# A whole row of output tile 36, instead of half a row, goes out by its own four small transfers

## The chip, the core and the metric

The kernel runs on one core of a Trainium2 chip, from one launch. The metric is the device time of an execution in microseconds (us), the median of several runs. The core has four compute engines that matter here (PE, the matmul engine; DVE, ACT and POOL, the elementwise engines), the engine SP, which only issues transfers, and 16 DMA engines that move data between the chip's main memory (HBM) and the on-chip memory of 128 partitions. DMAs that SP issues go through one queue (q1 in the profile), those that ACT issues through another (q10); every one of the 16 DMA engines serves both.

## What is computed

```python
x: (8, 12, 512, 64) float32      # batch, heads, rows t, channels c
y: (8, 12, 512, 64) float32
out = np.einsum('bhtc,bhsc->bhts', x, y)     # (8, 12, 512, 512) float32
```

These are 96 independent products, a 512x64 matrix by a 64x512 one. The inputs are 25.2 MB and the output is 100.7 MB, so most of the traffic is the output.

## The kernel before, in words

**Tiling.** The inputs come in twelve tiles of 128 partitions by 4096 float32 (16 KB a partition), six of x and six of y (`load`, line 129). ACT, DVE and POOL cast them to bfloat16 (`compress`, line 138), rearrange them (`mix`, line 162) and transpose them (`transposes`, line 177). The output is 48 tiles `o` of 128 partitions by 8 x 512 float32. A tile covers two heads. Partition p of it holds eight successive rows of one head, so that its 16 KB are one contiguous piece of HBM.

**One output tile** (`result`, line 259) is made in two halves, rows 0 to 3 and rows 4 to 7. For each half, PE does four matmuls of 128 by 512 (`products`, line 199, the matmul on line 205) into one of two PSUM buffers `pm0` and `pm1`. Then ACT copies the buffer into one of five `slot` buffers (line 115, the helper `copy`). In tiles 43 and 47 DVE copies in its place (line 117). After the second half the tile is stored by one DMA of 128 partitions by 16 KB (`store`, line 249, the issue on line 254): by SP, or, for every third tile and for the last four, by ACT, which then issues it after the first copy of the next tile.

**Order.** The program is written out by hand, tile after tile. `emit` (line 88) puts each operation on its engine's stream, and `need` (line 73) adds the semaphore waits that the buffers ask for. An engine runs its stream in order, so an operation that waits holds back all that stands behind it on that engine. A slot can be filled anew only when the DMA that stores it has landed.

**Tile 36 is the exception** (`SPLIT`, line 47). Its big store leaves out the last 256 of each partition's 4096 numbers (`size`, line 246), that is, the second half of the eighth row of every partition. These 128 pieces of 1 KB are computed again in another layout by `corner` (line 211), which `result` calls right after it has issued the big store. In `corner`:

- PE does eight matmuls (line 221) with 16 of the 128 rows each, by 256 columns, so that the result stands in 16 partitions by 2048 numbers of `pm0`.
- ACT copies that to `kept`, the first 16 partitions of a bfloat16 buffer that is no longer in use, `xk1` (line 230; the profile calls it xk<-pm).
- SP issues four DMAs (line 235). DMA r takes partitions r, r+4, r+8 and r+12 and writes eight pieces of 1 KB from each, 32 KB in all.

After that `result` goes on with tile 37. At the end of the program POOL waits for the four small DMAs (line 324), and the engines wait for the last store from each slot (lines 325 and 326).

Of the kernel before, what the change touches and what calls it, by code (L numbers as in the profile page):

```python
# [9 lines left out]
def kernel(  # L10
# [24 lines left out]
    _, _, S, _ = y.shape  # L35
    P = 128
    G = 16
# [5 lines left out]
    K = 8  # L43
# [1 line left out]
    D = 32  # L45
    SLOTS = 5
    SPLIT = 36
    W = S // 2
    fp32 = mybir.dt.float32
    bf16 = mybir.dt.bfloat16  # L50
    u32 = mybir.dt.uint32
# [5 lines left out]
    ov = out.rearrange("b h t s -> (b h t s)").rearrange(  # L57
        "(o u h q n) -> o h q u n", u=2, h=V, q=Q * E, n=K * S
    )
# [4 lines left out]
    xks = [sb.tile([P, R, C], bf16, name=f"xk{i}") for i in range(NG - 1)]  # L64
# [4 lines left out]
    pms = [ps.tile([P, 4, S], fp32, name=f"pm{i}") for i in range(2)]  # L69
# [18 lines left out]
    def emit(name, make, reads=(), writes=(), dma=None):  # L88

        points = [writer[r] for r in (*reads, *writes) if r in writer]  # L90
        points += [v for w in writes for v in readers.get(w, ())]
        if name == "pool" and name in ticks:
            points.append((name, ticks[name]))
        need(name, points)
        p, step = (name, 1) if dma is None else (f"dma{dma}", 16)
        if p not in sems:
            sems[p] = tc.alloc_semaphore(p)
        make().then_inc(sems[p], step)
        at = (p, ticks.get(p, 0) + step)
        ticks[p] = at[1]  # L100
        snaps[at] = {**known[name], p: at[1]}
        if dma is None:
            snaps[at][name] = at[1]
        for r in reads:
            readers.setdefault(r, []).append(at)
        for w in writes:
            writer[w], readers[w] = at, []
# [4 lines left out]
    def copy(name, dst, src, reads, writes):  # L112
        emit(
            name,
            lambda: nc.scalar.activation(dst, src, COPY)  # L115
            if name == "act"
            else engines[name].tensor_copy(dst, src),  # L117
            reads,
            writes,
        )  # L120
# [78 lines left out]
    def products(o, k):  # L199
        i, h = divmod(o, V)  # L200
        xT = xTs[i % 2].bitcast(bf16).rearrange("p (k h m) -> p k h m", k=K, h=V)
        yT = yTs[i % 2].bitcast(bf16)
        n = lambda j: min(S, size(o) - (k + j) * S)
        for j in range(4):
            last = nc.tensor.matmul(  # L205
                pms[k // 4][:, j, :n(j)], xT[:, k + j, h, :], yT[:, h * S:h * S + n(j)],
                start=True, stop=True,
            )
        return last

    def corner(o):

        i, h = divmod(o, V)
        xT = xTs[i % 2].bitcast(bf16).rearrange("p (k h m) -> p k h m", k=K, h=V)
        yT = yTs[i % 2].bitcast(bf16)
        kept = xks[1].bitcast(fp32).rearrange("p r c -> p (r c)")[:G, :]

        def make():

            for j in range(P // G):  # L220
                last = nc.tensor.matmul(  # L221
                    pms[0][:G, j // 2, j % 2 * W:(j % 2 + 1) * W],
                    xT[:, K - 1, h, j * G:(j + 1) * G],
                    yT[:, (h + 1) * S - W:(h + 1) * S],
                    start=True, stop=True,
                )
            return last

        emit("pe", make, [("xT", i % 2), ("yT", i % 2)], [("pm", 0)])
        copy("act", kept, pms[0].rearrange("p j s -> p (j s)")[:G, :], [("pm", 0)], [("xk", 1)])  # L230
        dst = ov[i, h].rearrange("(j a m) u n -> u m a j n", j=P // G, a=4)
        for r in range(4):
            emit(
                "sp",
                lambda: nc.sync.dma_start(
                    dst[r % 2, r // 2][:, :, K * S - W:],
                    kept[r::4].rearrange("p (j w) -> p j w", w=W),
                ),
                reads=[("xk", 1)],
                dma="corner",  # L240
            )
# [4 lines left out]
    def size(o):  # L246
        return K * S - W if o == SPLIT else K * S

# [10 lines left out]
    def result(o, s):  # L259

        for k in range(0, K, 4):
            pm = k // 4
            half = o // V % 2
            emit("pe", lambda: products(o, k), [("xT", half), ("yT", half)], [("pm", pm)])
            end = min(4 * S, size(o) - k * S)
            copy(
                "dve" if o in late else "act",
                slots[s][:, k * S:k * S + end],
                pms[pm].rearrange("p j s -> p (j s)")[:, :end],
                [("pm", pm)],  # L270
                [("slot", s, pm)],
            )
            if k == 0:
                while later:
                    store(*later.pop())
        if by_act(o):
            later.append((o, s))
        else:
            store(o, s)
        if o == SPLIT:  # L280
            corner(o)
# [75 lines left out]
```

## Time and profile before

| what | value |
|---|---|
| time, median of 3 runs | 300.77 us (300.7, 300.77, 301.01) |
| span of the profiled execution, first to last instruction | 298.9 us |
| what lies around the span, by the median of the runs | 1.87 us |
| bytes moved | 125.90 MB in 8789 packets, mean 421 GB/s |
| busiest compute engine | ACT, 205.4 us, 69% of the span |
| last landing of a transfer in the trace | 297.80 us |

The page gives no time of the profiled execution other than its span. So the 1.87 us is the difference between the median of the runs and the span, and it is taken to be the same for both kernels.

To read the profile: the slices on the page cut the span into 40 equal parts of 7.5 us and give the busy share of each engine in tenths. The DMA row is the mean over the 16 DMA engines. A DMA packet is one contiguous piece that one DMA engine moves; each transfer also has one packet of 4 bytes on every DMA engine that it uses, which reports the landing to a semaphore. The trace holds each packet's queue, start, duration and size, but not the number of its DMA engine.

### The profile page before, as it was taken

To read this page: it belongs to the slowest core of one execution; us is meant where nothing else is said; L and a number is where in the kernel's file an instruction comes from. 1 tells how busy PE (TensorE), PEld (TensorE's weight loads), DVE (VectorE), ACT (ScalarE), POOL (GpSimd) and SP (SyncE) were. 2 spreads that over 40 slices of the span, in tenths; PEclk is the share of its full clock that TensorE was granted. 3 is DMA by queue.
4 is the path that set the end of the run, shared out by engine and by line. 5 is a ranking of instruction groups with operands and counts; after the bars stand their busy time and mean duration, and the time that the engine had idled before them with its cause. 6 is when DMAs were issued, how large, how long until landed. Compare 5 with 4: busy or idle time off the path is not lost.

```text
span 298.9 us, 1185 instructions
## 1 busy us (share of the span) xinstructions
PE 128.5 (43%) x385; PEld 36.1 (12%) x392; DVE 160.7 (54%) x77; ACT 205.4 (69%) x106; POOL 56.1 (19%) x23
## 2 busy tenths in 40 slices
PE   0000040547566554464554555554653754567000
PEld 0000010111111111111111111111111211112000
DVE  2157897999839591920946719319377070500500
ACT  1665576999999876677776868685857994559000
POOL 2399999991000000000000000000000000000000
PEclk9999995657799979685979685959695799775655
DMA  7999999999999999999999999999999999999996
GB/s 274 430 423 439 430 428 423 428 439 428 425 436 432 425 425 442 428 428 432 432 428 433 434 428 425 436 425 428 434 434 425 422 433 419 423 428 425 430 434 259
DMA packets 8789, 125.90 MB, mean 421 GB/s; under 512 B 976, under 2 KB 1104, under 8 KB 1104
## 3 DMA queue, kind: packets, MB, share of 16 engines
q1 hardware_dynamic: 6192, 88.08, 69.4%
q10 hardware_dynamic: 2592, 37.75, 29.6%
q8 instruction: 3, 0.05, 0.1%
q14 instruction: 2, 0.02, 0.0%
HBM read 25.17 MB, written 100.66 MB: 421 GB/s over the span
## 4 chain that ended last, share of the span: by engine, by line
DMA 56%; ACT 22%; PE 7%; issue 5%; DVE 3%; SPq 0%; ACTq 0%
DMA out_dram<-slot 42%; ACT slot L115 19%; DMA slot<-in_y_dram 7%; DMA slot<-in_x_dram 6%; PE pm L205 6%; ACT xk L115 2%; DVE yb L117 2%; DVE slot L117 2%; ACT yb L115 1%; PE pm L221 1%; SPq L133 0%; ACTq L83 0%; SPq L352 0%; SPq L291 0%
## 5 line engine op out<-in xcount | busy, mean ns | idle before, releaser
L115 ACT ACTIVATE slot<-pm 128x2048 f32<-128x2048 f32 x92 | 166.0, 1884 | 47.9 <-DMA out_dram<-slot 38.2
L205 PE MATMUL pm<-yT,xT 128*128 128x512 bf16 x377 | 126.6, 475 | 144.3 <-ACT slot L115 96.3
L182 DVE STREAM_TRANSPOSE xT<-xb 128x2048 uint32<-128x2048 uint32 x12 | 46.7, 3888 | 75.3 <-PE pm L205 73.0
L205 PEld LDWEIGHTS pm<-yT,xT 128*128 128x128 bf16 x384 | 35.2, 111 | 235.4 <-ACT slot L115 134.9
L117 DVE COPY xb<-xk 32x2048 bf16<-32x2048 bf16 x36 | 46.9, 1302 | 1.0
L117 DVE CAST yb<-slot 64x2048 bf16<-64x2048 f32 x12 | 36.1, 3012 | 16.9 <-DMA slot<-in_y_dram 16.6
L117 POOL COPY xb<-xk 32x2048 bf16<-32x2048 bf16 x12 | 36.2, 3019 | 10.4 <-ACT xk L115 9.6
L115 ACT ACTIVATE xk<-slot 128x4096 bf16<-128x4096 f32 x6 | 21.7, 3617 | 16.3 <-DMA slot<-in_x_dram 16.2
L191 DVE STREAM_TRANSPOSE yT<-yb 128x1024 uint32<-128x1024 uint32 x12 | 23.1, 1922 | 0.0
L117 DVE COPY slot<-pm 128x2048 f32<-128x2048 f32 x4 | 9.0, 2286 | 25.3 <-PE pm L205 25.3
L115 ACT ACTIVATE yb<-slot 64x2048 bf16<-64x2048 f32 x6 | 14.8, 2461 | 5.1 <-DMA slot<-in_y_dram 5.1
L117 POOL CAST yb<-slot 64x2048 bf16<-64x2048 f32 x6 | 17.8, 2972 | 1.3 <-DMA slot<-in_y_dram 0.8
L221 PE MATMUL pm<-yT,xT 128*16 128x256 bf16 x8 | 1.9, 416 | 4.3 <-ACT slot L115 4.3
L297 DVE MEMSET xb<- 128x2048 uint32 x1 | 1.8, 1765 | 1.4 <-SPq L291 1.4
L115 ACT ACTIVATE xk<-pm 16x2048 f32<-16x2048 f32 x1 | 1.9, 1866 | 0.4 <-PE pm L221 0.4
L115 ACT ACT_TABLE_LOAD x1 | 1.3, 1283 | 0.9 <-SPq L291 0.9
L297 POOL MEMSET xb<- 128x2048 uint32 x1 | 1.8, 1804 | 0.5 <-SPq L291 0.5
L221 PEld LDWEIGHTS pm<-yT,xT 128*16 128x16 bf16 x8 | 0.9, 126 | 5.2 <-ACT slot L115 4.7
L341 POOL MEMSET const-float32-0.0<- 128x1 f32 x1 | 0.1, 97 | 0.2 <-issue 0.2
L341 POOL MEMSET const-float32-1.0<- 128x1 f32 x1 | 0.1, 98 | 0.0
L341 POOL MEMSET const-bfloat16-1.0<- 128x1 bf16 x1 | 0.1, 98 | 0.0
L341 POOL MEMSET const-uint8-127<- 128x1 uint8 x1 | 0.1, 98 | 0.0
## 6 DMA issues: line engine op xcount, KB each, us to landing
out_dram<-slot SPq DMA_DIRECT2D x29, 2048.0 KB, 16.6
out_dram<-slot ACTq DMA_DIRECT2D x18, 2048.0 KB, 14.7
slot<-in_x_dram SPq DMA_DIRECT2D x6, 2048.0 KB, 17.6
slot<-in_y_dram SPq DMA_DIRECT2D x6, 2048.0 KB, 20.8
out_dram<-slot SPq DMA_DIRECT2D x1, 1920.0 KB, 16.5
out_dram<-xk SPq DMA_DIRECT2D x4, 32.0 KB
```

Source lines behind the costliest of these rows:

```text
L115: lambda: nc.scalar.activation(dst, src, COPY)
L117: else engines[name].tensor_copy(dst, src),
L182: lambda: nc.vector.transpose(xTs[half].rearrange("p (k r e) -> p k e r", k=K, e=E), xbs[half].rearrange("p (k e c) -> p k e c", k=K, e=E),),
L191: lambda: nc.vector.transpose(yTs[half].rearrange("p (r j) -> p j r", r=D), ybs[half][b].rearrange("p (j c) -> p j c", c=D),),
L205: last = nc.tensor.matmul(pms[k // 4][:, j, :n(j)], xT[:, k + j, h, :], yT[:, h * S:h * S + n(j)], start=True, stop=True,)
L221: last = nc.tensor.matmul(pms[0][:G, j // 2, j % 2 * W:(j % 2 + 1) * W], xT[:, K - 1, h, j * G:(j + 1) * G], yT[:, (h + 1) * S - W:(h + 1) ...
L297: lambda: engines[name].memset(xbs[half], 0.0),
L341: nc = _bacc.Bacc("TRN2", target_bir_lowering=False, num_devices=1)
```

## The change

The piece that tile 36 gives away grows from half of the eighth row to all of it. The big store now carries 3584 numbers a partition (was 3840). The second half of tile 36 has three matmuls (was four, the last one 256 wide). `corner` does four matmuls of 32 rows by 512 columns (was eight of 16 by 256), and ACT copies 32 partitions by 2048 numbers (was 16 by 2048). Each of the four small DMAs takes eight partitions (was four), r, r+4 and so on to r+28, and writes four pieces of 2 KB from each (was eight of 1 KB): 64 KB a DMA, 256 KB in all (was 32 KB and 128 KB). No other tile is touched, no instruction changes its engine, and the order of the streams stays.

```diff
-    W = S // 2
+    W = S
+    M = 2 * G
...
-        n = lambda j: min(S, size(o) - (k + j) * S)
-        for j in range(4):
+        for j in range(min(4, size(o) // S - k)):
             last = nc.tensor.matmul(
-                pms[k // 4][:, j, :n(j)], xT[:, k + j, h, :], yT[:, h * S:h * S + n(j)],
+                pms[k // 4][:, j, :], xT[:, k + j, h, :], yT[:, h * S:(h + 1) * S],
                 start=True, stop=True,
             )
...
-        kept = xks[1].bitcast(fp32).rearrange("p r c -> p (r c)")[:G, :]
+        kept = xks[1].bitcast(fp32).rearrange("p r c -> p (r c)")[:M, :]
...
-            for j in range(P // G):
+            for j in range(P // M):
                 last = nc.tensor.matmul(
-                    pms[0][:G, j // 2, j % 2 * W:(j % 2 + 1) * W],
-                    xT[:, K - 1, h, j * G:(j + 1) * G],
-                    yT[:, (h + 1) * S - W:(h + 1) * S],
+                    pms[0][:M, j, :],
+                    xT[:, K - 1, h, j * M:(j + 1) * M],
+                    yT[:, h * S:(h + 1) * S],
                     start=True, stop=True,
                 )
...
-        copy("act", kept, pms[0].rearrange("p j s -> p (j s)")[:G, :], [("pm", 0)], [("xk", 1)])
-        dst = ov[i, h].rearrange("(j a m) u n -> u m a j n", j=P // G, a=4)
+        copy("act", kept, pms[0].rearrange("p j s -> p (j s)")[:M, :], [("pm", 0)], [("xk", 1)])
+        dst = ov[i, h].rearrange("(j a m) u n -> u m a j n", j=P // M, a=M // 4)
```

The loop over r with the four DMAs is unchanged. G is 16, S and T are 512, and `size(36)` is K * S - W.

## The prediction

> **What bounds the kernel now.** I read the page's slices first, then its DMA parts, then the stretches at the end, then the trace's packets one by one.
>
> ```profile
> span 298.9 us, 1185 instructions
> ...
> PE 128.5 (43%) x385; PEld 36.1 (12%) x392; DVE 160.7 (54%) x77; ACT 205.4 (69%) x106; POOL 56.1 (19%) x23
> ...
> DMA  7999999999999999999999999999999999999996
> ...
> DMA packets 8789, 125.90 MB, mean 421 GB/s; under 512 B 976, under 2 KB 1104, under 8 KB 1104
> ...
> q8 instruction: 3, 0.05, 0.1%
> ```
>
> No compute engine is above 69%, and the DMA row is at nine tenths from the second slice to the last but one. So the DMA engines bound the kernel. What matters is when the last of the 16 is through, and the mean hides that. The view of stretches shows it (columns: stretch, PE, PEld, DVE, ACT, POOL, clock, DMA share, GB/s):
>
> ```profile
> 290.00:295.00 5.00, 0.00 (x0) 0.00 (x0) 0.00 (x0) 0.00 (x0) 0.00 (x0) 0.50 1.02 433
> 295.00:296.00 1.00, 0.00 (x0) 0.00 (x0) 0.00 (x0) 0.00 (x0) 0.00 (x0) 0.50 0.73 311
> 296.00:297.00 1.00, 0.00 (x0) 0.00 (x0) 0.00 (x0) 0.00 (x0) 0.00 (x0) 0.50 0.35 147
> 297.00:298.90 1.90, 0.00 (x0) 0.00 (x0) 0.00 (x0) 0.00 (x0) 0.00 (x0) 0.50 0.00 0
> ```
>
> All 16 are busy to 295 us, then the share falls to 0.73 and 0.35: some end two microseconds before the others. To see which, I pulled the packets apart. On a busy DMA engine a packet starts 4 ns before its predecessor's end, and each engine must take eight data packets and one of 4 bytes from every 128-partition transfer. By these two rules the packets after 4.8 us fall into 16 sequences, none with a pause over 20 ns, and all with as many 16 KB packets. So nobody ever waits for work, and what an engine carries sets its end:
>
> ```
>                                                end of its last packet, us
> 4 engines with the small DMAs (32 packets each)  297.05 297.07 297.33 297.37
> 1 with PE's instruction packet of 187.2 us       297.34
> 1 with the one of 249.6 us                       297.22
> 1 with the one of 106.6 us                       296.25
> 2 with nothing special                           296.35 295.97
> 7 with nothing special                           295.59 to 295.72
> ```
>
> The q8 row above is these three instruction packets of 16 KB; the two late ones took 0.88 us each. So before, six engines share the end: the four with small DMAs, and two that also fetched PE's instructions. From 297.37 to the span's end, 298.91, is a tail of landing and closing that I keep.
>
> **The change part by part.** Prices are start to start on one engine, from the packets: 607 ns for 16 KB, 574 for 15 KB, 306 for 8 KB, 43 for 1 KB, 6 for 4 bytes.
>
> *Big store.* Each engine's eight packets shrink from 15 to 14 KB. A KB costs 33 ns between 15 and 16 KB and 38 between 8 and 15 KB, so 8 x 33 to 38 = 0.26 to 0.31 us less on **every** engine; I take 0.29.
>
> *Small DMAs.* The 976 packets under 512 B are 60 large transfers x 16 engines + 4 small ones x 4, and the 128 packets of 1 KB fill four sequences of 32: a DMA of four partitions runs on four engines, always the same. With eight partitions I expect eight. The four engines of before lose 32 x 43.5 + 4 x 6 = 1.42 us. Each of the eight gets 16 packets of 2 KB. No row has 2 KB; the bounds are two 1 KB packets (86 ns) and the 8 KB rate (77), and between the 1 and 8 KB rows a line gives 43 + 38 = 81, which I take. 16 x 81 + 4 x 6 = 1.32 us (1.26 to 1.40). [...]
>
> The sums:
> - the old four: -0.29 - 1.42 + 1.32 = -0.39 us, so 297.37 becomes 296.98
> - the four engines that are added: -0.29 + 1.32 = **+1.03 us**
> - the other eight: **-0.29 us**, so 297.34 becomes 297.05
>
> *Compute.* These are the rows around `corner`, from the timeline:
>
> ```profile
> 226.37 1.66 ACT L115 ACTIVATE slot<-pm 128x1792 f32<-128x1792 f32 x1
> ...
> 226.52 1.88 PE L221 MATMUL pm<-yT,xT 128*16 128x256 bf16 x8 [4.33 <-ACT slot L115]
> 228.44 1.87 ACT L115 ACTIVATE xk<-pm 16x2048 f32<-16x2048 f32 x1 [0.41 <-PE pm L221]
> 230.33 4.75 SPq L235 DMA_DIRECT2D out_dram<-xk  x4
> ```
>
> ACT's second copy of tile 36 goes from 1792 to 1536 wide. At (1884 - 1660)/256 ns a column that is 0.22 us less. The copy to `kept` keeps its 2048 columns, which set its 1.87 us. Four matmuls of 512 for eight of 256 have as many columns; bounds are half of 1.88 us and all of it, and I take 1.7. All of this lies beside DMA work: the transfer ahead, tile 36's own, is on the DMA engines until 241.6 us, 11 us after the copy. I cost it at nothing. Without that cover the chain would be about 0.4 us shorter.
>
> *SP's issues.* Four small ones take 4.75 us, 1.2 each, and the next store stands behind them, issued by 236.54. Engines without small packets reach its first packet at 241.57, right behind tile 36's last. An idle engine started 1.0 us after the first issue of the program, so 4 us are to spare. Eight partitions by four pieces are again 32 pieces; nothing to twice the time bounds it, I take the same, and even twice the time (+4.75 us, to 241.3, first packet 242.3) would overrun the shrunken store's end, 241.28, by only 1.0 us, with ACT's next store, issued at 239.5, to fill the hole. No wait is added: the last readers of `xk1` were done before 90 us. Tile 36's slot comes free 0.3 us sooner on most engines, which nobody lacks.
>
> **The rivals.** All turns on which engines are the added four. The profile doesn't number them.
>
> *Forecast: the two late fetchers are not among them.* The end goes from 297.37 to 297.05, so -0.32 us: 300.77 becomes **300.45**, the added ones ending at 295.7 + 1.03 = 296.7. If the engine of 296.35 is added it ends at 297.38, no change, 300.78; if that of 296.25, 297.28 and 300.68. All of it lies within 0.2% (0.6 us), about what a measurement of this kernel can tell from no change. [...]
>
> *Slower: a late fetcher is among them.* It would end at 297.34 + 1.03 = 298.37 or 297.22 + 1.03 = 298.25, so +1.00 or +0.88 us: **301.77 or 301.65**, +0.3%. It decides from the point where an added engine ended above 297.37 - 1.03 = 296.34 before, and costs more than 0.2% above 296.94. For it: of twelve engines outside the old four, two are late, and four drawn blindly miss both only in 8/12 x 7/11 = 42% of cases. Against it: the three instruction packets sat on three different engines, none of the old four. Number the engines so that the old four are 0 to 3 and the added ones 4 to 7. If successive packets go to successive engines, the first sits on one of ten places (4 to 13), and the second or third falls on 4 to 7 in three of them, 30%. I give both readings the same weight: 0.58 and 0.30 make 0.44.
>
> *The change doesn't spread.* If eight partitions still run on four engines, each has 32 packets of 2 KB, 2.62 us: -0.29 - 1.42 + 2.62 = +0.91, 301.68. The count of 976 speaks against it: small packets follow the partitions. On all 16 engines it would be 0.66 - 0.29 = +0.37 on a late fetcher, +0.34 us. Together 0.03, of which 0.02 slower.
>
> *SP's issue time doubles and nothing fills the hole:* +1.0 us on all engines, 300.45 + 1.0 = 301.45, slower; 0.01.
>
> **How the numbers follow.** Forecast 0.50. Late fetcher added 0.44, slower. No spread 0.02 slower, 0.01 within. Issue 0.01, slower. The rest, 0.02, is that the instruction packets lie elsewhere in the changed program (PE has ten instructions fewer before the third of them) and the end falls to the 296.7 of the others: -0.65 us, faster. So faster 0.02, within 0.51, slower 0.47. The time is that of the forecast, 300.45. Its own range is 300.25 to 300.85 (the bounds of 2 KB and 14 KB, and the sub-cases). Since the slower case holds nearly half, the range has to reach its upper price, 301.77 plus the 0.08 by which a 2 KB packet may be dearer: 300.25 to 301.85.
>
> **What would show it.** Packets under 512 B: 992 (60 x 16 + 4 x 8), and 992 + 128 = 1120 under 8 KB; another count says how far the small DMAs spread. Bytes stay 125.90 MB. In the stretches at the end, the forecast has a share near zero from 297.05 on; the slower case has one engine, a share of some 0.06, to 298.3. The packets show it best: eight sequences with 16 packets of 2 KB, and where the instruction packets sit. I am wrong in the step, not only in the case, if a 2 KB packet takes well over 86 ns, if an engine pauses around 241 us, or if the old four are not among the eight.

## The result, and the profile after

The changed kernel is slower: 301.56 us (median of ten runs, 301.38 to 301.92) against 300.83 (ten runs, 300.7 to 301.01), a ratio of 1.0025 with a 95% interval of 1.0016 to 1.0034. That is +0.73 us where -0.32 had been forecast. The time lies in the range, but the forecast case was not the one that came. The profiled execution is the slowest of the ten, 301.92 us.

These are lines of the page of the changed kernel:

```profile
span 300.1 us, 1175 instructions
...
DMA packets 8805, 125.90 MB, mean 419 GB/s; under 512 B 992, under 2 KB 992, under 8 KB 1120
...
out_dram<-slot SPq DMA_DIRECT2D x1, 1792.0 KB, 15.8
out_dram<-xk SPq DMA_DIRECT2D x4, 64.0 KB
```

The counts are those that eight partitions on eight engines give: 992 landing packets and 128 pieces of 2 KB. The bytes are the same. The rows around `corner` in the timeline:

```profile
226.64 1.45 ACT L116 ACTIVATE slot<-pm 128x1536 f32<-128x1536 f32 x1
...
226.80 1.89 PE L221 MATMUL pm<-yT,xT 128*32 128x512 bf16 x4 [4.66 <-ACT slot L116]
...
228.73 1.87 ACT L116 ACTIVATE xk<-pm 32x2048 f32<-32x2048 f32 x1 [0.64 <-PE pm L221]
230.62 5.05 SPq L235 DMA_DIRECT2D out_dram<-xk  x4
```

ACT's copy is 0.21 us shorter, PE takes as long as before, and SP's four issues take 0.3 us more. Nothing here explains 0.73 us. The last stretches do (columns: stretch, PE, PEld, DVE, ACT, POOL, clock, DMA share, GB/s; a packet is counted in the stretch in which it starts):

```profile
295.00:296.00 1.00, 0.00 (x0) 0.00 (x0) 0.00 (x0) 0.00 (x0) 0.00 (x0) 0.50 0.58 246
296.00:297.00 1.00, 0.00 (x0) 0.00 (x0) 0.00 (x0) 0.00 (x0) 0.00 (x0) 0.50 0.39 164
297.00:298.00 1.00, 0.00 (x0) 0.00 (x0) 0.00 (x0) 0.00 (x0) 0.00 (x0) 0.50 0.08 33
298.00:300.10 2.10, 0.00 (x0) 0.00 (x0) 0.00 (x0) 0.00 (x0) 0.00 (x0) 0.50 0.00 0
```

From 297 us on one DMA engine works alone: the share is near 1/16. Before, several engines shared the end. The packets, pulled apart as in the prediction, name it:

```
                                                   end of its last packet, us
8 engines with 16 packets of 2 KB: one at          298.56
                                   the other seven 296.66 to 296.91
PE's instruction packet of 251.8 us                296.95
the ones of 178.7 and 106.8 us                     296.17, 296.02
5 with nothing special                             295.40 to 295.66
```

That the packets of queue q8 hold PE's instructions is an estimate: no view says whose they are, but in the traces of the two kernels PE starts 226 to 265 instructions (rows PE and PEld) between one such packet and the next, every other compute engine at most 55. Two sequences whose packets end at the same moment can't be told apart from there on. So the ends of 296.91 and 296.95 may be exchanged; nothing below turns on it.

So no fetcher is among the eight, which was the condition of the forecast. Seven of the eight end where the sums put them (296.7 to 297.0). The eighth carries no packet of its own. Its 16 KB packets are longer. Let the **excess** of an engine be what its 16 KB packets take beyond 611 ns, the duration that most of them have, in the sum. From 62 to 240 us it has 2.04 us of it, in delays of mostly 3 to 23 ns on three packets in four (7 ns on the mean of some 290), and the other seven have at most 0.5 us. It begins with the stores, 180 us ahead of the small DMAs. In the trace of before one engine has the same habit, from 62 to 190 us, 1.31 us in the sum: the one that ended at 296.35 us.

### The profile page after: what moved, and what is told of

Read it like the earlier page. It is cut to its first block, busy times and chain, and to the rows that moved or that the text cites. A ratio compares the mean times of both kernels' runs of the same rounds, so it can differ in the third digit from the quotient of the medians.

```text
span 300.1 us, 1175 instructions
## 1 busy us (share of the span) xinstructions
PE 126.7 (42%) x380; PEld 34.9 (12%) x387; DVE 160.7 (54%) x77; ACT 205.2 (68%) x106; POOL 56.1 (19%) x23
## 4 chain that ended last, share of the span: by engine, by line
DMA 56%; ACT 22%; PE 6%; issue 5%; DVE 3%; SPq 0%; ACTq 0%
DMA out_dram<-slot 43%; ACT slot L116 20%; DMA slot<-in_y_dram 7%; DMA slot<-in_x_dram 6%; PE pm L205 6%; ACT xk L116 2%; DVE yb L118 2%; DVE slot L118 1%; ACT yb L116 1%; PE pm L221 1%; SPq L134 0%; ACTq L84 0%; SPq L352 0%; SPq L291 0%
## 5 line engine op out<-in xcount | busy, mean ns | idle before, releaser
L205 PE MATMUL pm<-yT,xT 128*128 128x512 bf16 x376 | 124.9, 469 | 147.0 <-ACT slot L116 106.1
L205 PEld LDWEIGHTS pm<-yT,xT 128*128 128x128 bf16 x383 | 34.4, 110 | 237.3 <-ACT slot L116 139.2
L221 PE MATMUL pm<-yT,xT 128*32 128x512 bf16 x4 | 1.9, 628 | 4.7 <-ACT slot L116 4.7
L116 ACT ACTIVATE xk<-pm 32x2048 f32<-32x2048 f32 x1 | 1.9, 1866 | 0.6 <-PE pm L221 0.6
```

Of the source, the lines that this page charges most:

```text
L205: last = nc.tensor.matmul(pms[k // 4][:, j, :], xT[:, k + j, h, :], yT[:, h * S:(h + 1) * S], start=True, stop=True,)
L221: last = nc.tensor.matmul(pms[0][:M, j, :], xT[:, K - 1, h, j * M:(j + 1) * M], yT[:, h * S:(h + 1) * S], start=True, stop=True,)
```

## The experiments

**Theory:** one DMA engine is slower than the others in every execution; it is among the added four, and its 1.03 us set the end. **Rival A:** which engine is slow is chance, or any four added engines cost as much. **Rival B:** the small transfers, or SP's issues, slow an engine down. Where no other count is given below, a time is that of a single run.

### Numbering the engines: ruler_before and ruler_after

```diff
+    marks = sb.tile([16, 16, 32], fp32, name="marks")
...
+    def ruler():
+        k = len(marked) + 1
+        if k < 16:
+            marked.append(k)
+            emit(
+                "sp",
+                lambda: nc.sync.dma_start(marks[:k, k, :], xv[0][:k, :32]),
+                writes=[("mark", k)],
+                dma="ruler",
+            )
...
             store(o, s)
+            ruler()
```

> The kernel before, with 15 marks added: behind 15 of its stores SP issues one more small load of k partitions by 128 B, k = 1 to 15, into a buffer that nobody reads. A DMA of k partitions runs on the first k DMA engines, so the number of marks in an engine's sequence of packets tells its number: engine e has 15 - e. Theory: one engine among numbers 4 to 7 moves every 16 KB packet of the stores more slowly than the others from the first store on (the one that ended at 296.35 us before the change, with a steady 11 ns a packet and no packet of its own). It shows again here, with the same habit, on a number from 4 to 7, and ends between 296.4 and 297.5 us, hidden below the old four and the late fetchers. Rival A (it is a chance which engine is slow in an execution): the slow one has any number, or there is none. Rival B (the small transfers of the change slow an engine): no engine is slow here. The marks cost engine 0 about 15 x 20 ns = 0.3 us, so 301.0 us in time by all theories.

> The changed kernel with the same 15 marks. Theory: the slow engine has the same number from 4 to 7 as in the marked kernel before; its excess begins with the stores at some 62 us and not with the small DMAs at 241 us, and it ends last, at 297.9 to 298.8 us; the three instruction packets of PE lie on engines 8 to 15. Time 301.4 to 302.1 us. Rival A: the slow engine is another one, and if it is outside 0 to 7 the time is 300.5 to 300.8. Rival B: the excess begins at the small DMAs.

Measured: 301.05 us for the marked kernel before and 302.01 for the marked changed one, each beside 301.0 for the kernel before. The marks number the 16 sequences: engine e is the one with 15 - e of them. In both the one with the steady excess has 11 marks: **engine 4**, with 2.0 and 2.1 us from 62 to 240 us. In the marked changed kernel engines 0 to 7 carry the small packets and engine 4 ends at 298.58 us, the other seven at 296.69 to 297.23. In the marked kernel before it ends at 297.69, with the old four at 297.25 to 297.67. PE's instruction packets sit on engines 12 and 13, in both, and the third on 14 in the marked changed kernel (in the other the sequences can't be told apart surely at that point). What follows: the slow engine is the same one in both, and in the marked changed kernel the fetchers lie outside engines 0 to 7.

### Without small DMAs, and with seven partitions: whole36 and drop7

```diff
-    SPLIT = 36
+    SPLIT = -1
```

> The kernel before without any exception for tile 36: it is stored whole by one DMA, with no small DMAs. Every engine carries the same bytes. Theory: each engine ends 0.27 us later than in the kernel before, but the four with small DMAs 1.15 us sooner: the late fetchers at 297.6 and 297.5 us set the end, or the slow engine if it is slow enough in this execution (up to 297.8); about 301.1 us. Rival B: no engine with a steady excess, as there are no small transfers.

Measured: 301.07 us. One engine has an excess of 2.0 us from 62 to 240 us and ends at 297.71; the last fetcher ends at 297.74, the other fetchers at 296.84 and 296.55, and the rest at 295.91 to 296.36. There are no small transfers here, so rival B's slow engine can't come from them.

```diff
-                    dst[r % 2, r // 2][:, :, K * S - W:],
-                    kept[r::4].rearrange("p (j w) -> p j w", w=W),
+                    dst[r % 2, r // 2][:7, :, K * S - W:],
+                    kept[r:28:4].rearrange("p (j w) -> p j w", w=W),
```

> The changed kernel, but each small DMA takes only seven of its eight partitions; the rows of the eighth (16 of the 128 pieces of 2 KB) are left unwritten. Seven partitions run on seven engines, so the highest of the eight engines is spared and nothing else changes. Theory, if the slow engine is the highest of the eight: it carries 1.32 us less, the end goes to that of the fetchers and the old four, some 297.0 us, 300.3 to 300.5 us in time, faster than both kernels. If it is another of the added four: as the changed kernel, 301.4 to 301.9. Rival B (small transfers slow the engines that they run beside): the end stays near 298 us, because seven engines still carry them.

Measured: 301.76 us, as the changed kernel. I had hoped that the slow engine was the highest of the eight, number 7, and that this would free it. It wasn't: the engine with the excess keeps its 16 packets and ends at 298.35. The other six, engines 5 and 6 among them (the mark of seven partitions went to engines 0 to 6), carry the same 16 packets and end by 297.2, so it is not enough to be an added engine. Taking the wrong engine's share away is worth nothing.

### Engine 4 alone: drop4 and drop5

The same edit, with `[:4, ...]` and `kept[r:16:4]`, and with `[:5, ...]` and `kept[r:20:4]`.

> The changed kernel, but each small DMA takes only the first four of its eight partitions; the rows of the others (64 of the 128 pieces of 2 KB) are left unwritten. So engines 0 to 3 carry their 16 small packets as in the changed kernel, and 4 to 7 carry none. Theory: engine 4 sets the end of the changed kernel; without its 16 packets (1.32 us) it ends at some 297.2 us, beside the late fetchers, and the time is 300.3 to 300.6 us, 1.0 to 1.2 below the changed kernel. To be read together with the run in which engine 4 keeps its share. Rival A (any four added engines cost the time): also faster. Rival B (it is the length of the small transfers or SP's issue): still 301.4 to 301.7, since the same four DMAs are issued.

> As the run with four of the eight partitions, but with five: 48 of the 128 pieces are left unwritten, and the only difference to the run with four is that engine 4 carries its 16 small packets. Theory: engine 4 alone brings back the whole loss, 301.3 to 301.8 us, as the changed kernel, 0.8 to 1.3 us above the run with four. Rival A (each of the four added engines costs its part): a quarter of the loss, 0.2 to 0.3 us above the run with four. Rival B: no difference between the two.

Measured, in ten runs each: 300.41 us (300.36 to 300.82) with four partitions, ratio to the kernel before 0.9987 (0.9978 to 0.9997), and 301.68 (301.43 to 302.05) with five, 1.0029 (1.0019 to 1.0038). The two kernels differ by 16 packets of 2 KB, all on engine 4, and by **1.27 us**, close to the 1.34 us that the packets take. These are the packet count and the last stretches, with four partitions:

```profile
DMA packets 8725, 125.77 MB, mean 421 GB/s; under 512 B 976, under 2 KB 976, under 8 KB 1040
```

```profile
296.00:297.00 1.00, 0.00 (x0) 0.00 (x0) 0.00 (x0) 0.00 (x0) 0.00 (x0) 0.50 0.23 98
297.00:298.00 1.00, 0.00 (x0) 0.00 (x0) 0.00 (x0) 0.00 (x0) 0.00 (x0) 0.50 0.00 0
```

and with five:

```profile
DMA packets 8745, 125.80 MB, mean 419 GB/s; under 512 B 980, under 2 KB 980, under 8 KB 1060
```

```profile
296.00:297.00 1.00, 0.00 (x0) 0.00 (x0) 0.00 (x0) 0.00 (x0) 0.00 (x0) 0.50 0.19 82
297.00:298.00 1.00, 0.00 (x0) 0.00 (x0) 0.00 (x0) 0.00 (x0) 0.00 (x0) 0.50 0.08 33
```

The five-partition kernel has 20 packets more (16 and 4 landings). They sit on the engine that works alone after 297 us, which is missing in the other kernel. In the packets, engine 4 ends at 297.13 and 298.32. That settles the cause of the loss, engine 4's 16 packets: rival A would have a quarter of the loss here, rival B none.

### The kernel before again: again_before

> The kernel before, unchanged, for a second trace of it. In the first trace the slow engine lost its excess at 190 us and ended at 296.35 us; in the marked kernel before and in the one without the exception it kept it to 240 us. Theory: the long form is the usual one, so here the engine that has the excess, and carries no packet of its own, ends at 297.3 to 297.6 us, level with the old four and the late fetchers, and the time is 300.7 to 301.0 us. Rival: the short form belongs to the kernel before; then it ends at 296.2 to 296.5 us again.

Measured: 300.67 us beside 300.64. The engine with the excess ends at 297.33 us, with 2.04 us of excess from 62 to 240 us; the old four and the last fetcher end at 297.06 to 297.38. So the first trace, on which the prediction rests, shows engine 4 about 1 us earlier than it usually is. (These two traces have no marks; the engine is known by its excess.) Of the twelve traces of this study in which its excess can be read, it ends well before 240 us in two, that one and the one of `block` below. The fetchers move too: the one whose packet started at 187.2 us ended at 297.34 in the first trace, and here the one of 186.7 us ends at 296.51.

One thing more stands in the packets. Engine 4 is not alone in having an excess. In this trace and in that of the changed kernel, most other engines begin to have one between 180 and 240 us, and from 240 to 280 us it is as large as engine 4's: 0.3 to 0.4 us in these 40 us. What sets engine 4 apart is that it begins at 62 us. In the changed kernel's trace the fetchers of 106.8 and 178.7 us have none from 240 to 280 us, and in the first trace of the kernel before engine 4 has none there either.

### Whose slowness it is: ruler_whole, block and halves

`ruler_whole` is whole36 with the marks; `block` changes only where it writes:

```diff
+    obv = out.rearrange("b h t s -> (b h t s)").rearrange("(o p n) -> o p n", p=P, n=K * S)
...
-            lambda: engines[name].dma_start(ov[i, h][:, :, :size(o)], slots[s][:, :size(o)]),
+            lambda: engines[name].dma_start(obv[o], slots[s]),
```

> The kernel without the exception for tile 36, with the marks that number the engines; the partner of the run in which the stores go to other addresses. Theory: engine 4 has the steady excess of some 11 ns a packet from the first stores to 240 us and ends at 297.7 to 298.0 us, with engine 14 near it; the others have none. 301.0 to 301.4 us. Rival (chance decides which engine is slow): another number.

> The same, but each output tile is stored as one contiguous block of 2 MB, partition after partition, so that the rows of the output stand in wrong places (every byte is written once). [...] Theory: the slowness belongs to engine 4 or its partitions, so engine 4 has the same excess, 2.2 to 2.7 us in the sum, and the time stays at 301.0 to 301.6 us. Rival: it comes from the addresses that engine 4's partitions write to; then its excess goes away, or another engine has it, and engine 4 ends with the others at 295.9 to 296.4 us.

Measured: 301.37 and 301.42 us. In both, the sequence with 11 marks has the excess (1.7 and 1.6 us from 62 to 240 us), and the other sequences have at most 0.2 us of it before 200 us, but for 0.1 to 0.6 us around instruction packets. So the excess stays with engine 4 when the addresses in HBM change. What is left is engine 4 itself, or the eight partitions whose 16 KB pieces it moves in a store; which eight these are no trace shows.

```diff
+        for part in range(2):
             emit(
                 name,
-                lambda: engines[name].dma_start(ov[i, h][:, :, :size(o)], slots[s][:, :size(o)]),
+                lambda: engines[name].dma_start(
+                    ov[i, h][part * 32:(part + 1) * 32, :, :size(o)],
+                    slots[s][part * 64:(part + 1) * 64, :size(o)],
+                ),
```

> The changed kernel with the marks that number the engines, and with each large store cut in two DMAs of 64 partitions. [...] Theory: the slowness belongs to DMA engine 4 itself: engine 4 has the steady excess again (some 11 ns a 16 KB packet from the first stores to 240 us), the other 15 have none. [...] The time is about that of the marked changed kernel, 302.0 us, plus 48 more landing packets an engine at 6 ns (0.3 us) and what 48 more issues cost, 302.0 to 303 us.

Measured: 427.81 us. The DMA engines stay busy (a share of 0.95 to 1.01 in three stretches between 60 and 350 us) but move far less:

```profile
span 426.0 us, 1245 instructions
...
DMA packets 9815, 125.93 MB, mean 296 GB/s; under 512 B 2000, under 2 KB 2000, under 8 KB 2128
```

A 16 KB packet takes 608 to 1961 ns, so an excess of 7 ns (the expectations had put it at 11) can't be read. 302.0 to 303 us had been expected; the run is inconclusive, and whether it is the engine or its partitions stays open.

### Past the slow engine with POOL's DMAs: pool7

```diff
+            k = 9 if r else 5
...
+                lambda: nc.gpsimd.dma_start(marks[:k, r, :], xv[0][:k, :32]),
...
+                lambda: nc.gpsimd.dma_start(
+                    dst[r % 2, r // 2][:7, :, K * S - W:],
+                    kept[r:28:4].rearrange("p (j w) -> p j w", w=W),
+                ),
...
+                lambda: nc.sync.dma_start(
+                    dst[r % 2, r // 2][7:, :, K * S - W:],
+                    kept[28 + r:29 + r].rearrange("p (j w) -> p j w", w=W),
+                ),
```

> The whole eighth row as in the changed kernel, all of it written, but 112 of its 128 pieces go out by four DMAs of seven partitions that POOL issues, each behind a dummy load of 5 (the first) or 9 partitions by 128 B; the other 16 pieces go out by four SP DMAs of one partition, which should run on engines 0 to 3, one piece each. The aim is the seven engines 5 to 11, past the slow one. Theory: if POOL's DMAs take successive engines, 5 to 11 carry 16 packets of 2 KB and end at 296.4 to 296.8, engines 0 to 3 at 296.3, engine 4 at 297.2, the fetchers at 297.0: 300.3 to 300.6 us, 0.1% to 0.2% below the kernel before. [...] If they begin at engine 0 each time, engine 4 has them again: 301.4 to 301.8 us. Rival B (the small transfers as such slow the end): 301.4 or more in either case.

Measured: 302.23 us (301.99 to 302.56), 1.0045 (1.003 to 1.006): slower than both. Two things failed. POOL's data went out as 56 packets of 4 KB. Each DMA put two of them on each of seven engines; but the four DMAs did not use the same seven, so the packets are spread over most of the engines, some four each. That POOL's DMAs take successive engines from 5 on, which the plan rested on, is not shown. The engine with the excess has four and ends at 298.16 us: it was not spared. And the 16 pieces that SP's one-partition DMAs wrote took 0.12 to 0.69 us each, 0.45 on the mean, against 0.08 in the changed kernel. They sit on four engines, and these end at 298.04 to 298.67 us. So the loss is one of the means, and says nothing for or against sparing engine 4.

No complete version beat the kernel before. The four-partition kernel does, but it leaves half of the eighth rows of tile 36 unwritten. SP's small DMAs of four, five, seven and eight partitions put their packets on as many engines here, engine 4 among them from five on, so of these only four partitions spare it, which is what the kernel before has; and in `again_before` its old four, engine 4 and the last fetcher end within 0.33 us of each other, so little is left there.

## Why the prediction was wrong

- **What bounds the kernel**: right. No compute engine and no wait came into it (ACT, the busiest, has 68% of the span); the end, at 298.56 us, is that of the last DMA engine.
- **Big store, -0.29 us**: right. A 14 KB packet takes 536 ns on the mean against 575 for 15 KB, 8 x 39 = 0.31.
- **Small DMAs, 1.32 us on each of eight engines**: right. A 2 KB packet takes 82 ns on the mean (81 assumed): 16 x 82 + 4 x 6 = 1.34.
- **The old four are among the eight**: right. The sums rest on it, and no run before the change shows it. The marked runs do: the small packets sit on engines 0 to 7 in the marked changed kernel, and the old four are among these.
- **Compute and SP's issues at nothing**: right. The end shows no pause on engine 4 over 20 ns, and with the same four DMAs issued, dropping three of their eight partitions left the time where it was, and dropping a fourth, engine 4's, took 1.27 us off.
- **The forecast case**: its condition held. No late fetcher was added; PE's packets lie on engines 12, 13 and 14, the "successive" reading of the rival. But its price was wrong. The step that failed is the sub-case "if the engine of 296.35 is added it ends at 297.38, no change". The mechanism was that one, and the size was mis-read: 296.35 came from one trace in which that engine was slow for 130 us. Usually it is slow for 180 us and ends at about 297.33, level with the others (`again_before`). 297.33 + 1.03 = 298.36 would have given +0.99 us; the changed kernel's trace, of its slowest run, has 298.56, and the medians differ by 0.73.
- **The slower rival** had the right sign, place and rule (an added engine that ended late), and named the wrong one: a fetcher in place of engine 4. The measured time lies in the range because the range was stretched to this rival's price. As the rival did not come, that is luck.
- The chances gave the slower side 0.47. The engine of 296.35 ended 0.7 us after seven others with nothing special, and I took that for a fixed number; I did not ask from when to when it was late, nor whether another execution would show it longer.

Open: why engine 4 has its excess from the first store on and the others only much later, why it stops earlier in some executions, and whether its partitions have a part in it.

## What to carry to other kernels

When all DMA engines are busy almost to the end, as here (a share of 1.03 from 290 to 295 us in the changed kernel), the time is that of the engine that is through last, and the mean share hides it: pull the packets apart by engine, then ask of every late engine what made it late and whether that is the same in another execution. A small DMA of four, five, seven or eight partitions, issued by SP, put its packets on as many engines here, engine 4 among them from five on, so a choice of four or eight partitions is a choice of who pays. An engine that looks only a little late in one trace may be at the edge in the next: engine 4 ended at 296.35 us in one trace of the kernel before and at 297.33 in the other.

## What the runs showed of the hardware that was not expected

- Engine 4 has 1.3 to 2.1 us of excess in the 180 us from 62 to 240 us, in every trace where it can be read (it is numbered in four of them, from two chips), and no more than the others while the inputs are loaded, with the output at two different sets of addresses. From 240 us on most of the others have it at the same rate, 0.3 to 0.4 us in 40 us.
- PE's instruction packets of 16 KB go to successive engines, 12, 13 and 14, in three marked runs (in the fourth only 12 and 13 are sure), and each takes 0.88 to 0.97 us. In the traces of the two kernels their engines end 0.4 to 1.7 us after most of those with nothing special.
- Stores of 64 partitions in place of 128, two for one, cut the mean rate from 419 GB/s (the marked changed kernel) to 296, though all 16 engines take part; no run here shows why.
- Four engines that take pieces of one and the same partition needed 0.45 us for 2 KB in `pool7`, five times the usual 0.08; no run separates the shared partition from another cause.
